# A transformer block on one core: in the last matrix product, the transfer of the second weight sum is put first and its use one product later, and product 2 is summed in two PSUM banks of its own

## The chip, the cores and the metric

The kernel runs on one core of a Trainium2 chip. The metric is the device time of one execution in microseconds (us); smaller is better. A profile adds one execution with every instruction's start, length and waits.

## The reference

One layer of a decoder block, batch 1, 512 tokens, width 1024, everything in float32:

```python
h = rmsnorm(x, norm_attn_g)
[q | k | v | u_pool | u_gate] = h @ w_in
a = diff_attention(q, k, v, ...)          # 8 heads, causal
p = multiscale_pool(u_pool, ...)
x = x + (sigmoid(g_A) * a + sigmoid(g_P) * p) @ w_out
z = square(relu(rmsnorm(x, norm_mlp_g) @ w_up))     # w_up 1024 x 4096
x = x + z @ w_down                                   # w_down 4096 x 1024
out = rmsnorm(x, final_norm_g)
```

The change lies in the last three lines.

## The kernel before

**Precision.** Every float32 product is made of three passes of TensorE: an operand is split into a high part (`hi`, a cast to the narrower float32r by ScalarE) and a low part (`lo`, the remainder, by VectorE), and hi x hi, lo x hi and hi x lo are summed. So each weight block needs a cast on ScalarE (ACT, line 112) and a subtraction on VectorE (DVE, line 113) before TensorE (PE) may use it, and so does each block of z (lines 694 and 695).

**The MLP in four quarters.** The 4096 hidden columns are done in quarters `q` = 0 to 3: `up(q)` computes z of a quarter (quarter 0 by the plain `up_plain`), `down(q)` multiplies it with its quarter of `w_down` and adds it to `x1`. Each is a 2 x 2 block product by a scheme of Strassen's kind: seven products of sums of blocks in place of eight. The products are named m1 to m7 in the code, and each takes a weight form: m5 takes S1, m1 takes A11, m2 takes A12, m6 takes S2, m3 takes S4, m7 takes S3, m4 takes A22. The text says "product 5" for m5, and so on. A product of `down` is 24 matmuls of 128 x 512 (two banks, four slices, three passes).

**Weights.** `weights` makes the weight forms of a quarter. Four blocks are in HBM, each as two halves of 128 x 1024 (512 KB), numbered by `c`. Blocks 0 and 1 are loaded over SyncE's queue (SP) into `r11` (buffers `wr`) and `al` (`wal`). Their sum `ga` (`wga`, line 665) is the form S1, the first weight sum. Other forms are made in place by DMAs that add while they write, issued on GpSimd's queue (POOL, line 645): `al` + block 3 is S3, `ga` + block 3 is S2 (the second weight sum), and `ga` + block 2 is A22's. Before such an addition may start, the low part of the form that is there must have been taken out of the buffer. Blocks 2 (A12) and 3 (S4) are loaded as they are into the two `wr` buffers, so each load waits until the buffer's last user is through.

```python
for n, form in enumerate(order):
    if n == 1:
        plus(al, 3)
    ...
        w = parts(ga, f"t{form}", None if form == S1 else first[-1])
        if form != A22:
            plus(ga, {S1: 3, S2: 2}[form])
```

In a group name, `wh_dt` and `wl_dt` are the high and low part of a weight sum of `down` (`wh_ut` of `up`), `wh_db` and `wl_db` those of a block used as it is. A name with numbers says which: `wh_dt5_1_0` is the form S2 (code 5) of quarter 1, half 0; `wh_db21_1_0` is block 2 (for product 2) of quarter 1, half 0. `z0`, `z1`, `z4`, `z5` are z for A11, A12, S1, S2.

**PSUM.** `acc` hands out the eight banks in turn. A product's two banks are added to `x1` by DVE (`to_x1`, line 837); products 1, 6, 7 and 4 go on in the same two banks (`ma`), 5 and 3 in another pair (`mc`), and product 2 takes a fresh pair in each quarter and is added to `x1` in each.

**Order.** The program is written product by product, and a scheduler with a timeline of its own then sets the order of the instructions on each engine; `after(later, earlier)` only adds a rule of order. On the chip, each engine runs its own list in that order: an instruction that waits holds up all that stand behind it on its engine.

Of the kernel before, what the change touches and what calls it, by code (L numbers as in the profile page):

```python
# [15 lines left out]
ALU = mybir.AluOpType  # L16
# [35 lines left out]
def block_kernel(ctx, tc, xT, x_tok, gains, pos, consts, w_in, w_v, w_pool, w_out, w_up, w_dn, out):  # L52
# [5 lines left out]
    def after(later, earlier):  # L58
        tc.add_manual_dep(
            later.ins, earlier.ins.name,  # L60
            mybir.DependencyInfo(mybir.DependencyClass.NoSync, mybir.DependencyReason.DATA), reason="issue order",
        )
# [252 lines left out]
    acc = Rot((0, 1, 2))  # L315
# [310 lines left out]
        parts(S4)  # L626


    nparts = [0]
    first = []  # L630
    zform = {}

    def weights(src, q, nm, order):

        def raw(b, tag="wr", pool=wp):
            tiles = [pool.tile([P, 1024], F32, tag=tag, name=f"{tag}_{nm}{b}_{q}_{c}", bufs=2) for c in range(2)]
            if b is not None:
                for c in range(2):
                    nc.sync.dma_start(out=tiles[c], in_=src[q, b, c])
            return tiles  # L640

        def plus(tiles, b):

            for c in range(2):
                G.dma_start(out=tiles[c], in_=src[q, b, c], accum_op=ALU.add)  # L645

        def parts(rs, b, hold=None):

            third = nparts[0] % 3 == 2
            nparts[0] += 1  # L650
            out_ = []
            for c in range(2):
                hi, lo = (
                    (bk if third else wp).tile([P, 1024], F32R, tag=t_ + "b" * third, name=f"{t_}_{nm}{b}_{q}_{c}", bufs=2 if third else 4)
                    for t_ in ("wh", "wl")
                )
                cast = split_w(rs[c], hi, lo, eng=V)
                if hold:
                    after(cast, hold)
                out_.append((hi, lo))  # L660
            return out_

        r11, al, ga = raw(0), raw(1, "wal", bk), raw(None, "wga", bk)
        for c in range(2):
            V.tensor_tensor(out=ga[c], in0=r11[c], in1=al[c], op=ALU.add)  # L665
        for n, form in enumerate(order):
            if n == 1:
                plus(al, 3)
            if form == A11:
                yield parts(r11, "b11")  # L670
            elif form == A12:
                yield parts(raw(2), "b21")
            elif form == S4:
                yield parts(raw(3), "b22")
            elif form == S3:
                yield parts(al, "t3", first[-1])
            else:
                w = parts(ga, f"t{form}", None if form == S1 else first[-1])
                if form != A22:
                    plus(ga, {S1: 3, S2: 2}[form])  # L680
                yield w

    def halves(r):
# [22 lines left out]
    def up_plain(q):  # L706

        rows = state["rows"]
        for c in range(2):
            for par in range(2):  # L710
                w = []
                for kh in range(2):
                    tiles = load_w(w_up[q, 2 * kh + par, c], f"up{q}_{kh}{par}{c}")
                    cast = split_w(*tiles, eng=V)
                    if c + par:
                        after(cast, rows)
                    w.append(tiles[1:])
                pa = [acc(f"pu{q}_{par}{c}_{p}") for p in range(2)]
                for ts in ((0, 1), (1, 2)) if c + par == 0 else ((0, 2),):
                    for p in range(2):  # L720
                        a_ = pa[p][:, ts[0] * HS : ts[1] * HS]
                        for part in range(2):
                            for k in range(NK):
                                c_ = slice((p * 4 + k % 4) * P, (p * 4 + k % 4) * P + P)
                                for i in range(2 - part):
                                    T.matmul(a_, lhsT=w[k // 4][part][:, c_], rhs=gab[k // 4][:, ts[0] : ts[1], i, k % 4, :],  # L726
                                             start=k + i + part == 0, stop=part == 1 and k == NK - 1)
                for p in range(2):
                    r = rawz[:, (0, 1)[par] : (4, 3)[par] : (3, 1)[par], 2 * c + p, :]
                    A.activation(out=r, in_=pa[p].rearrange("p (a t) -> p a t", a=2), func=AF.Relu)  # L730
                    A.activation(out=r, in_=r, func=AF.Square)
                if c + par == 0:
                    forms_h2()
            sub(4, 2, 3, c)
            zsplit(q, S1, R[4], c)
            zsplit(q, A11, R[0], c)
            sub(4, 4, 0, c, True)
            zsplit(q, S2, R[4], c)
            zsplit(q, A12, R[1], c)
            sub(1, 4, 1, c, True)  # L740
            sub(0, 0, 3, c)
        zsplit(q, S4, R[1])
        zsplit(q, S3, R[0])
        zsplit(q, A22, R[2])

    def up(q):

        W = weights(w_up, q, "u", (A11, S1, S2, S3, A22, A12, S4))

        def product(form, name, onto=None):  # L750
            w, pa = next(W), onto or [acc(f"u{name}{q}_{i}") for i in range(2)]
            rh, rl = gf[form]
            first.append(None)
            for i in range(2):
                hi, lo = w[i]
                for p in range(2):
                    a_ = pa[i][:, p * HS : p * HS + HS]
                    for k in range(4):
                        c = slice((p * 4 + k) * P, (p * 4 + k) * P + P)
                        m = T.matmul(a_, lhsT=hi[:, c], rhs=rh[:, k, :], start=p + k == 0 and onto is None, stop=False, skip_group_check=True)  # L760
                        first[-1] = first[-1] or m
                        T.matmul(a_, lhsT=hi[:, c], rhs=rl[:, k, :], start=False, stop=False, skip_group_check=True)  # L762
                    for k in range(4):
                        c = slice((p * 4 + k) * P, (p * 4 + k) * P + P)
                        T.matmul(a_, lhsT=lo[:, c], rhs=rh[:, k, :], start=False, stop=k == 3, skip_group_check=True)  # L765
            return pa

        def keep(pa, r):
            for a_, r_ in zip(bank_view(pa), halves(r)):
                A.copy(out=r_, in_=a_)  # L770

        def join(pa, r):
            for a_, r_ in zip(bank_view(pa), halves(r)):
                V.tensor_tensor(out=r_, in0=a_, in1=r_, op=ALU.add)

        def z_of(r, sign, pa=None):
            for i, r_ in enumerate(halves(r)):
                A.activation(out=r_, in_=bank_view(pa)[i] if pa else r_, func=AF.Relu, scale=sign)
                A.activation(out=r_, in_=r_, func=AF.Square)

        ma = product(A11, "m1")
        keep(ma, R[0])
        mc = product(S1, "m5")
        keep(mc, R[2])
        product(S2, "m6", onto=ma)
        keep(ma, R[1])
        product(S3, "m7", onto=ma)
        join(ma, R[2])
        z_of(R[2], -1.0)
        product(A22, "m4", onto=ma)  # L790
        z_of(R[3], 1.0, ma)
        sub(4, 2, 3)
        zsplit(q, S1, R[4])
        join(product(A12, "m2"), R[0])
        z_of(R[0], 1.0)
        zsplit(q, A11, R[0])
        sub(4, 4, 0, neg=True)
        zsplit(q, S2, R[4])
        product(S4, "m3", onto=mc)
        join(mc, R[1])  # L800
        z_of(R[1], -1.0)
        zsplit(q, A12, R[1])
        sub(1, 4, 1, neg=True)
        zsplit(q, S4, R[1])
        sub(0, 0, 3)
        zsplit(q, S3, R[0])
        zsplit(q, A22, R[2])

    def down(q):
        W = weights(w_dn, q, "d", (S1, A11, S2, A12, S4, S3, A22))  # L810
        last = q == 3

        def mms(a_, form, w, a, cols, start):
# [11 lines left out]
        def product(form, name, onto=None):  # L825
            w, pa = next(W), onto or [acc(f"d{name}{q}_{a}") for a in range(2)]
            first.append(None)
            for a in range(2):
                m, _ = mms(pa[a], form, w, a, (0, 512), onto is None)
                first[-1] = first[-1] or m  # L830
            return pa

# [16 lines left out]
        to_x1(mc, 1, 1)  # L849
        ma = product(A11, "m1")  # L850
        to_x1(ma, 0, 0)
        product(S2, "m6", onto=ma)
        if last:
            after(gmul, first[-1])
        to_x1(ma, 0, 1)
        to_x1(product(A12, "m2"), 0, 0)
        complete(0, 0)
        product(S4, "m3", onto=mc)
        to_x1(mc, 0, 1)
        if last:  # L860
# [104 lines left out]
```

## Time and profile before

| what | value |
|---|---|
| median of 3 runs | 704.28 us (702.53 to 705.14) |
| profiled execution, its time | 700.6 us |
| profiled execution, its span | 698.8 us |
| TensorE busy in the span | 678.3 us (97%) |
| VectorE / ScalarE / GpSimd busy | 519.1 / 446.1 / 161.8 us |
| mean granted TensorE clock | 0.991 |
| read from HBM | 100.30 MB, 147 GB/s over the span |

The span runs from the first to the last instruction; the time of the same execution is 1.8 us longer. TensorE's busy time counts a matmul from its issue to its modelled end, so that neighbours overlap: 97% busy leaves little room, and what there is shows as stretches in which TensorE waits or runs at a lower granted clock. The MLP's four `down` parts begin at about 402, 480, 563 and 646 us.

### The profile page before, as it was taken

The numbers are of one execution on the slowest core, as the hardware profiler recorded it, in microseconds if no ns is written. First come the engines' busy times: TensorE is split into PE (matmuls) and PEld (weight loads), VectorE is DVE, ScalarE is ACT, GpSimd is POOL, SyncE is SP. The second block draws the span as 40 slices with busy tenths as digits, with TensorE's granted clock in tenths as the row PEclk, the third lists the DMA queues.
The fourth block names the chain that finished last, engine by engine and source line by source line (L and its number), as shares of the span: only waits on it lengthen the run. The fifth ranks groups of instructions, "written<-read, shape, count | busy, mean of one in ns | idle before, by whom it ended". The sixth has DMA issues, their size and how long they took to land.

```text
span 698.8 us, 9783 instructions
## 1 busy us (share of the span) xinstructions
PE 678.3 (97%) x3590; PEld 581.6 (83%) x3590; DVE 519.1 (74%) x853; ACT 446.1 (64%) x723; POOL 161.8 (23%) x159
## 2 busy tenths in 40 slices
PE   8999999999999999999999999999899999999795
PEld 7888878887888887888888888999689978899584
DVE  6943977688788865965489789468985789567796
ACT  8554487877888789874356665366545765267555
POOL 6101634264346524610000100102010110101000
PEclk9999999999999999999999999999999999999999
DMA  8534573416346274584133774879468784876723
GB/s 276 170 106 124 133 151 111 110 60 151 103 117 151 69 174 91 121 240 170 42 121 99 141 206 129 173 219 209 128 185 186 194 183 164 187 182 162 178 61 120
DMA packets 30863, 103.03 MB, mean 147 GB/s; under 512 B 3808, under 2 KB 4448, under 8 KB 30816
## 3 DMA queue, kind: packets, MB, share of 16 engines
q1 hardware_dynamic: 21456, 68.59, 28.7%
q0 software_dynamic: 9216, 33.56, 27.5%
q8 instruction: 28, 0.46, 0.3%
q10 hardware_dynamic: 144, 0.26, 0.1%
q14 instruction: 19, 0.16, 0.1%
HBM read 100.30 MB, written 2.10 MB: 147 GB/s over the span
## 4 chain that ended last, share of the span: by engine, by line
PE 68%; DVE 13%; DMA 8%; ACT 6%; issue 4%; POOL 1%; SPq 0%; ACTq 0%; POOLq 0%; DVEq 0%
PE pu L726 5%; PE dm L821 5%; PE dm L822 5%; PE dm L819 5%; DMA wga_dNone<-w_dn 3%; PE um L760 3%; PE um L762 3%; PE um L765 3%; PE v L220 2%; PE v L221 2%; PE v L222 2%; DMA wga_uNone<-w_up 2%; PE po L557 2%; PE po L558 2%; PE po L559 2%
## 5 line engine op out<-in xcount | busy, mean ns | idle before, releaser
L821 PE MATMUL dm<-wh_dt,z 128*128 128x512 f32 (+1 forms) x128 | 49.6, 387 | 0.1
L822 PE MATMUL dm<-wl_dt,z 128*128 128x512 f32 (+1 forms) x128 | 49.2, 386 | 0.0
L819 PE MATMUL dm<-wh_dt,z 128*128 128x512 f32 (+1 forms) x128 | 48.9, 388 | 0.3 <-ACT z L694 0.3
L837 DVE TENSOR_TENSOR x<-x,dm 128x512 f32<-128x512 f32 x54 | 36.3, 681 | 15.0 <-PE dm L822 14.9
L112 ACT CAST wh_ut<-wga_uNone 128x1024 fp32r<-128x1024 f32 x18 | 18.9, 1050 | 43.3 <-DMA wga_uNone<-w_up 32.5
L376 ACT ACTIVATE p<-p,st 128x128 f32<-128x128 f32 (+3 forms) x64 | 35.7, 559 | 12.4 <-DVE st L372 11.8
L821 PE MATMUL dm<-wh_db,z 128*128 128x512 f32 x96 | 39.3, 417 | 4.3 <-DVE z L695 4.3
L819 PE MATMUL dm<-wh_db,z 128*128 128x512 f32 x96 | 38.2, 409 | 3.8 <-ACT wh_db L112 3.1
L112 ACT CAST wh_dt<-wga_dNone 128x1024 fp32r<-128x1024 f32 x24 | 24.9, 1047 | 22.7 <-DMA wga_dNone<-w_dn 17.6
L113 DVE TENSOR_TENSOR wl_ut<-wga_uNone,wh_ut 128x1024 fp32r<-128x1024 f32 x18 | 22.0, 1223 | 23.2 <-ACT wh_ut L112 23.2
L113 DVE TENSOR_TENSOR wl_dt<-wga_dNone,wh_dt 128x1024 fp32r<-128x1024 f32 x24 | 28.9, 1219 | 13.3 <-ACT wh_dt L112 13.3
L645 POOL DMA_DIRECT2D wal_d<-w_dn x8 | 6.9, 864 | 135.3 <-DVE wga_dNone L665 118.9
L822 PE MATMUL dm<-wl_db,z 128*128 128x512 f32 x96 | 38.0, 408 | 0.0
L112 ACT CAST wh_db<-wr_d 128x1024 fp32r<-128x1024 f32 x24 | 25.0, 1045 | 19.2 <-DMA wr_d<-w_dn 17.8
L760 PE MATMUL um<-gss,wh_ut 128*128 128x256 f32 x144 | 36.1, 283 | 0.0
L762 PE MATMUL um<-gss,wh_ut 128*128 128x256 f32 x144 | 36.1, 283 | 0.0
L113 DVE TENSOR_TENSOR wl_db<-wr_d,wh_db 128x1024 fp32r<-128x1024 f32 x24 | 29.1, 1218 | 7.2 <-PE pu L726 4.5
L695 DVE TENSOR_TENSOR z<-rawz,z 128x1024 fp32r<-128x1024 f32 (+1 forms) x32 | 34.2, 1084 | 0.0
L726 PE MATMUL pu<-gab,wh_up 128*128 128x512 f32 (+1 forms) x160 | 31.7, 349 | 0.6 <-DVE gab L596 0.4
L372 DVE CUSTOM_DVE_ANT_0 p<-s,mask 128x128 f32<-128x128 f32 (+3 forms) x64 | 29.8, 482 | 2.0 <-PE s L371 2.0
L694 ACT CAST z<-rawz 128x1024 fp32r<-128x1024 f32 (+1 forms) x32 | 29.3, 937 | 2.9 <-PE dm L822 1.2
L726 PEld LDWEIGHTS pu<-gab,wh_up 128*128 128x128 f32 x160 | 25.9, 189 | 5.0 <-DVE gab L596 0.8
(310 smaller groups left out, 2235.2 us busy)
## 6 DMA issues: line engine op xcount, KB each, us to landing
wr_d<-w_dn SPq DMA_DIRECT2D x24, 512.0 KB, 3.6
wr_u<-w_up SPq DMA_DIRECT2D x18, 512.0 KB, 3.8
wga_dNone<-w_dn POOLq DMA_DIRECT2D x16, 512.0 KB, 5.7
wga_uNone<-w_up POOLq DMA_DIRECT2D x12, 512.0 KB, 7.9
wr_q<-w_in SPq DMA_DIRECT2D x8, 512.0 KB, 3.3
wr_k<-w_in SPq DMA_DIRECT2D x8, 512.0 KB, 3.7
wr_ga<-w_in SPq DMA_DIRECT2D x8, 512.0 KB, 3.3
wr_gp<-w_in SPq DMA_DIRECT2D x8, 512.0 KB, 3.3
```

The lines of the kernel that those rows point to most:

```text
L112: ins = A.copy(out=hi[:, sl], in_=raw[:, sl])
L113: (eng or G).tensor_tensor(out=lo[:, sl], in0=raw[:, sl], in1=f(hi)[:, sl], op=ALU.subtract)
L372: V.tensor_tensor_reduce(out=pr[:, c, :N], in0=s_[:, :N], in1=mask[:, S - N :], scale=-0.125, scalar=-NEG, op0=ALU.add, op1=ALU.min, accum ...
L376: A.activation(out=pr[:, c, :N], in_=pr[:, c, :N], func=AF.Exp, scale=-1.0, bias=st[:, c : c + 1], accum_out=st[:, 2 + c : 3 + c])
L695: V.tensor_tensor(out=z[:, 1, sl], in0=r[:, sl], in1=f(z[:, 0, sl]), op=ALU.subtract)
L726: T.matmul(a_, lhsT=w[k // 4][part][:, c_], rhs=gab[k // 4][:, ts[0] : ts[1], i, k % 4, :], start=k + i + part == 0, stop=part == 1 and k ...
L760: m = T.matmul(a_, lhsT=hi[:, c], rhs=rh[:, k, :], start=p + k == 0 and onto is None, stop=False, skip_group_check=True)
L762: T.matmul(a_, lhsT=hi[:, c], rhs=rl[:, k, :], start=False, stop=False, skip_group_check=True)
L819: m = T.matmul(a_, lhsT=zh, rhs=hi[:, sl], start=p == 0 and start, stop=False, skip_group_check=True)
L821: T.matmul(a_, lhsT=zl, rhs=hi[:, sl], start=False, stop=False, skip_group_check=True)
L822: end = T.matmul(a_, lhsT=zh, rhs=lo[:, sl], start=False, stop=p == 3, skip_group_check=True)
L837: V.tensor_tensor(out=xs, in0=xs, in1=pa[a], op=(ALU.add, ALU.subtract)[n])
```

## The change

In `weights`, which `up` and `down` share, the addition of block 3 to `ga` (which makes the second weight sum) is issued ahead of the addition of block 3 to `al`; `after` ties that order. In `down`, product 2 (A12) is written ahead of product 6 (S2), and in `up` the split of z for A12 ahead of that for S2. Product 2's two banks are now banks 6 and 7, kept for it alone: it is summed over the four quarters there and added to `x1` once, in the last quarter; `acc` turns over the six others.

```diff
+    acc = Rot(tuple(range(6)))
+    m2 = [bank(6 + a, f"dm2_{a}") for a in range(2)]
...
         def plus(tiles, b):
-            for c in range(2):
-                G.dma_start(out=tiles[c], in_=src[q, b, c], accum_op=ALU.add)
+            return [G.dma_start(out=tiles[c], in_=src[q, b, c], accum_op=ALU.add) for c in range(2)]
...
         for n, form in enumerate(order):
-            if n == 1:
-                plus(al, 3)
...
                 w = parts(ga, f"t{form}", None if form == S1 else first[-1])
                 if form != A22:
-                    plus(ga, {S1: 3, S2: 2}[form])
+                    adds = plus(ga, {S1: 3, S2: 2}[form])
+                if form == S1:
+                    for i in plus(al, 3):
+                        after(i, adds[1])
                 yield w
...
# up_plain
             zsplit(q, A11, R[0], c)
+            zsplit(q, A12, R[1], c)
             sub(4, 4, 0, c, True)
             zsplit(q, S2, R[4], c)
-            zsplit(q, A12, R[1], c)
...
# up
         zsplit(q, A11, R[0])
-        sub(4, 4, 0, neg=True)
-        zsplit(q, S2, R[4])
         product(S4, "m3", onto=mc)
         join(mc, R[1])
         z_of(R[1], -1.0)
         zsplit(q, A12, R[1])
+        sub(4, 4, 0, neg=True)
+        zsplit(q, S2, R[4])
...
# down
-        W = weights(w_dn, q, "d", (S1, A11, S2, A12, S4, S3, A22))
+        W = weights(w_dn, q, "d", (S1, A11, A12, S2, S4, S3, A22))
...
-                m, _ = mms(pa[a], form, w, a, (0, 512), onto is None)
+                m, _ = mms(pa[a], form, w, a, (0, 512), onto is None or onto is m2 and q == 0)
...
         ma = product(A11, "m1")
         to_x1(ma, 0, 0)
-        product(S2, "m6", onto=ma)
+        product(A12, "m2", onto=m2)
         if last:
             after(gmul, first[-1])
+            to_x1(m2, 0, 0)
+        complete(0, 0)
+        product(S2, "m6", onto=ma)
         to_x1(ma, 0, 1)
-        to_x1(product(A12, "m2"), 0, 0)
-        complete(0, 0)
         product(S4, "m3", onto=mc)
```

What the scheduler makes of it shows at three places, all in quarter 1 of `down` (quarter 2 has the same rows). First POOL's list, the six additions of the quarter, before:

```order
L645 DMA wal_d1_1_0_4475<-w_dn 128x1024
L645 DMA wga_dNone_1_0_4479<-w_dn 128x1024
L645 DMA wal_d1_1_1_4476<-w_dn 128x1024
L645 DMA wga_dNone_1_1_4480<-w_dn 128x1024
L645 DMA wga_dNone_1_0_4479<-w_dn 128x1024
L645 DMA wga_dNone_1_1_4480<-w_dn 128x1024
```

and now:

```order
L646 DMA wga_dNone_1_0_4477<-w_dn 128x1024
L646 DMA wga_dNone_1_1_4478<-w_dn 128x1024
L646 DMA wal_d1_1_0_4473<-w_dn 128x1024
L646 DMA wal_d1_1_1_4474<-w_dn 128x1024
L646 DMA wga_dNone_1_0_4477<-w_dn 128x1024
L646 DMA wga_dNone_1_1_4478<-w_dn 128x1024
```

Both additions to `wga` that make the second weight sum now stand ahead of both additions to `wal`. Then ACT's list, from the cast of z for A11 (`z0`) on, before (the rows 778 and 779 are ReLU and square of z):

```order
L694 CAST z0_1_4384<-rawz_2995 128x1024
L778 ACTIVATE rawz_2995<-rawz_2995 128x512
L112 CAST wh_dt5_1_0_4559<-wga_dNone_1_0_4479 128x1024
L112 CAST wh_dt5_1_1_4563<-wga_dNone_1_1_4480 128x1024
L779 ACTIVATE rawz_2995<-rawz_2995 128x512
L778 ACTIVATE rawz_2995<-rawz_2995 128x512
L694 CAST z5_1_4388<-rawz_2995 128x1024
L779 ACTIVATE rawz_2995<-rawz_2995 128x512
L112 CAST wh_db21_1_0_4599<-wr_d2_1_0_4595 128x1024
L694 CAST z1_1_4457<-rawz_2995 128x1024
L112 CAST wh_db21_1_1_4603<-wr_d2_1_1_4596 128x1024
```

and now, from the row ahead of ReLU and square:

```order
L112 CAST wh_db21_1_0_4561<-wr_d2_1_0_4557 128x1024
L781 ACTIVATE rawz_2995<-rawz_2995 128x512
L782 ACTIVATE rawz_2995<-rawz_2995 128x512
L781 ACTIVATE rawz_2995<-rawz_2995 128x512
L697 CAST z0_1_4382<-rawz_2995 128x1024
L782 ACTIVATE rawz_2995<-rawz_2995 128x512
L781 ACTIVATE rawz_2995<-rawz_2995 128x512
L782 ACTIVATE rawz_2995<-rawz_2995 128x512
L112 CAST wh_db21_1_1_4565<-wr_d2_1_1_4558 128x1024
L697 CAST z1_1_4451<-rawz_2995 128x1024
L697 CAST z5_1_4455<-rawz_2995 128x1024
L112 CAST wh_dt5_1_0_4593<-wga_dNone_1_0_4477 128x1024
```

The casts of the second weight sum (`wh_dt5`) have moved from ahead of z for A12 (`z1`) to behind it, and the first cast of product 2's weights (`wh_db21_1_0`) has moved ahead of `z0`. In quarter 3 that cast stays behind `z0`, and `wh_dt5` moves as here. Third, PE's list at the end of product 1 of quarter 1, before:

```order
L819 MATMUL dm11_1_4532<-wh_db11_1_1_4527,z0_1_4384 128x512
L821 MATMUL dm11_1_4532<-wh_db11_1_1_4527,z0_1_4384 128x512
L822 MATMUL dm11_1_4532<-wl_db11_1_1_4528,z0_1_4384 128x512
L819 MATMUL dm21_0_4607<-wh_db21_1_0_4599,z1_1_4457 128x512
L819 MATMUL dm21_1_4608<-wh_db21_1_0_4599,z1_1_4457 128x512
L821 MATMUL dm21_0_4607<-wh_db21_1_0_4599,z1_1_4457 128x512
```

and now:

```order
L822 MATMUL dm11_1_4530<-wh_db11_1_1_4525,z0_1_4382 128x512
L824 MATMUL dm11_1_4530<-wh_db11_1_1_4525,z0_1_4382 128x512
L825 MATMUL dm11_1_4530<-wl_db11_1_1_4526,z0_1_4382 128x512
L822 MATMUL dm2_0_3357<-wh_db21_1_0_4561,z1_1_4451 128x512
L822 MATMUL dm2_1_3358<-wh_db21_1_0_4561,z1_1_4451 128x512
L824 MATMUL dm2_0_3357<-wh_db21_1_0_4561,z1_1_4451 128x512
```

Here nothing moved: in quarters 1 to 3 the scheduler had put product 2 right behind product 1 already before the change. Only its banks are others.

## The prediction

> **What bounds the kernel now.** I read the page's first part, then the waits by engine, then stretches of the `down` parts.
>
> ```profile
> PE 678.3 (97%) x3590; PEld 581.6 (83%) x3590; DVE 519.1 (74%) x853; ACT 446.1 (64%) x723; POOL 161.8 (23%) x159
> PE dm L821 <- DVE z L695: 4.3, 3, 1.9
> PE dm L819 <- ACT wh_db L112: 3.1, 1, 3.1
> ACT wh_dt L112 <- DMA wga_dNone<-w_dn: 17.6, 5, 5.2
> ```
>
> TensorE is the bound, so only its own waits are worth anything. The two largest (total us, times, longest) are in `down`: it waits for z's low part three times and once for a cast of weights. Idle time is not all that such a wait costs. A `down` product is 24 matmuls, so I set product 1 of quarters 1, 2 and 3 beside the product 2 that follows it (stretch, its length, PE busy, granted clock, DMA share, GB/s):
>
> ```profile
> 485.71:491.15 5.44, 5.44 (x25) 1.00 0.70 109
> 491.16:501.14 9.98, 7.62 (x25) 0.83 0.69 186
> 568.73:574.17 5.44, 5.44 (x25) 1.00 0.78 126
> 574.18:583.32 9.14, 7.32 (x25) 0.81 0.62 190
> 652.36:657.80 5.44, 5.44 (x25) 1.00 0.66 153
> 657.81:669.18 11.37, 7.73 (x25) 0.85 0.65 153
> 494.50:497.90 3.40, 3.40 (x10) 0.59 0.76 258
> ```
>
> The same 24 matmuls take 5.44 us undisturbed, and 9.98, 9.14 and 11.37 us in product 2. The excess is 4.54, 3.70 and 5.93 us, 14.17 us in all. Some of it is idle, the rest a lower granted clock: 0.59 in the 3.4 us behind the wait of quarter 1. Who is late there shows ACT's timeline, with PE's two waits behind it (start, length, engine, line):
>
> ```profile
> 486.30 1.05 ACT L112 CAST wh_dt<-wga_dNone 128x1024 fp32r<-128x1024 f32 x1 [5.25 <-DMA wga_dNone<-w_dn]
> 487.26 0.63 ACT L779 ACTIVATE rawz<-rawz 128x512 f32<-128x512 f32 x1
> ...
> 490.73 1.04 ACT L694 CAST z<-rawz 128x1024 fp32r<-128x1024 f32 x1
> 491.81 0.73 PE L819 MATMUL dm<-wh_db,z 128*128 128x512 f32 x2 [0.50 <-ACT z L694]
> 494.40 0.50 PE L821 MATMUL dm<-wh_db,z 128*128 128x512 f32 x1 [1.86 <-DVE z L695]
> ```
>
> ACT stands still for 5.25 us at the second half of `wh_dt5`, because the addition that makes this weight sum has not landed. ReLU, square and cast of z for A12 (490.73) stand behind it in ACT's list, though product 2 needs nothing of that sum. PE pays at 491.81 and 494.40. Why the sum is late, POOL's timeline shows. Behind it stand SP's issue of the first load for product 2, the page's row of all additions (packets, MB, share of the DMA engines' time), and landings (us from the issue, the last figure): the addition issued at 476.86, one with POOL's queue to itself, the load issued at 474.32, and an undisturbed load:
>
> ```profile
> 469.62 0.86 POOL L645 DMA_DIRECT2D wal_d<-w_dn  x1 [16.83 <-DVE wga_dNone L665]
> 471.72 0.86 POOL L645 DMA_DIRECT2D wga_dNone<-w_dn  x1 [1.25 <-DVE wl_dt L113]
> 472.86 0.86 POOL L645 DMA_DIRECT2D wal_d<-w_dn  x1 [0.27 <-DVE wga_dNone L665]
> 476.86 0.86 POOL L645 DMA_DIRECT2D wga_dNone<-w_dn  x1 [3.14 <-DVE wl_dt L113]
> 474.32 0.33 SPq L639 DMA_DIRECT2D wr_d<-w_dn  x1
> ...
> q0 software_dynamic: 9216, 33.56, 27.5%
> wga_dNone<-w_dn POOLq DMA_DIRECT2D x1, 512.0 KB, 9.4
> wga_dNone<-w_dn POOLq DMA_DIRECT2D x1, 512.0 KB, 5.2
> wr_d<-w_dn SPq DMA_DIRECT2D x1, 512.0 KB, 9.5
> wr_d<-w_dn SPq DMA_DIRECT2D x1, 512.0 KB, 3.2
> ```
>
> The addition behind two to `wal` takes 9.4 us, one alone 5.2. All additions together, 64 of 512 KB, take 27.5% of 698.8 us on the DMA engines, 3.0 us each, which is my pace for a row of them. Quarters 2 and 3 look alike.
>
> **The change part by part, and the sum.**
>
> *Additions reordered.* POOL's list now has both `wga` additions first. Each still waits for the low part taken out of `wga` (the releaser in their rows), so neither can start earlier than 471.72 and 476.86. The first then lands at about 471.72 + 5.2 = 477, the second at 476.86 + 5.2 = 482, at worst 1.5 us later beside a load, not at 486.3. The `wal` additions come behind: two at 3.0 us each put the last at about 488 to 490. In `down` nothing reads `wal` before product 7, which starts 16 us (three products of 5.44) after product 2's start at 491.16, so I take 0; in `up` there is a case for a loss, the last rival.
>
> *Casts reordered.* z for A12 and its weights no longer stand behind `wh_dt5`. PE's list shows no gain of its own, since product 2 already followed product 1 there. The gain is that its operands come in time. In quarter 1, ACT ends the first cast of product 2's weights at about 479.5 (landing 474.32 + 3.2, and up to 1 us more beside the addition still in flight), then ReLU, square, ReLU and `z0` bring it to about 483, three more ReLU and squares (0.63 each) to 485, the second weight cast and `z1` to 487.5, the low part on DVE to about 489. Product 2 begins at 491.16. I take its excess as gone in quarters 1 and 2: 4.54 + 3.70. `wh_dt5` then ends near 490; product 6 wants it at 496.6. For each quarter the ends are nothing and the whole excess.
>
> *Quarter 3.* The excess of 5.93 goes too, but this part is short of DVE:
>
> ```profile
> 646.00:691.00 45.00, 37.31 (x55) 0.96 0.41 101
> 651.57 1.05 ACT L112 CAST wh_dt<-wga_dNone 128x1024 fp32r<-128x1024 f32 x1 [4.24 <-DMA wga_dNone<-w_dn]
> 655.38 1.05 ACT L112 CAST wh_dt<-wga_dNone 128x1024 fp32r<-128x1024 f32 x1 [2.76 <-DMA wga_dNone<-w_dn]
> ```
>
> ACT stood for 7 us here. DVE is busy 37.31 of 45.00 us; with 5.93 us less it would be 37.31 of 39.07, 95%. I take 4.8 and leave 1.1 to a queue that has little room; the ends are 0 and 5.93.
>
> *Product 2's own banks.* Six additions to `x1` fall away (two in each of quarters 0 to 2). By this row they take 6 x 0.681 = 4.1 us off DVE:
>
> ```profile
> L837 DVE TENSOR_TENSOR x<-x,dm 128x512 f32<-128x512 f32 x54 | 36.3, 681 | 15.0 <-PE dm L822 14.9
> 481.09 0.68 DVE L774 TENSOR_TENSOR rawz<-um,rawz 128x512 f32<-128x512 f32 x1
> 481.69 1.22 DVE L702 SCALAR_TENSOR_TENSOR rawz<-rawz 128x1024 f32<-128x1024 f32 x1
> ```
>
> They lie beside TensorE, and DVE waits 15.0 us for PE ahead of this group, so I take 0 (ends 0 and 4.1). Six banks in turn for eight: product 1 of `down` now takes the banks of product 3's sum in `up`, which the addition at 481.09 reads. It ends at 481.8 and product 1 begins at 485.7, so 0; with DVE held up it costs what is beyond 3.9 us.
>
> The sum: 4.54 + 3.70 + 4.8 = 13.0 us off the profiled execution, 700.6 to 687.6. The runs' median is 3.7 us above that execution; I take the same 13.0 off it: 704.28 - 13.0 = **691.3 us**.
>
> [...]
>
> **The rivals.**
>
> *The wait moves to product 1.* The first cast of product 2's weights now stands ahead of `z0` in quarters 1 and 2. If its load lands as late as now, 474.32 + 9.5 = 483.8, then cast (1.05), low part (1.2), join (0.68), subtraction and `z0`'s low part (1.22 each) end at 489.2, where product 1 wants it at about 486.4: 2.8 us idle and some 2 of slow clock, all that quarter 1 loses now. Quarter 2 likewise, quarter 3 not. The time would be 704.28 - 4.8 = 699.5. Against it: at 474.32 only one addition is now in POOL's queue, not three. [...]
>
> *DVE binds quarter 3.* If 95% cannot be had and only 1 of the 5.93 us goes, the time is 704.28 - 4.54 - 3.70 - 1 = 695.0. For it speaks that DVE's list is in order and the casts it waits for come from ACT; against it, that ACT's 7 us held DVE up too, so that part of its rows comes earlier.
>
> *Nothing changes:* the loads and additions are the same bytes, DMA decides and the waits go to other casts, 704.3. Against it: ACT's 5.25 us and 7 us are waits for a sum that the next product does not use.
>
> *Slower.* In `up`, `wal` is read by product 7, and its casts now wait for additions that stand last:
>
> ```profile
> 437.91 0.86 POOL L645 DMA_DIRECT2D wga_uNone<-w_up  x1 [1.77 <-DVE wl_ut L113]
> 451.22 2.01 ACT L112 CAST wh_ut<-wal_u 128x1024 fp32r<-128x1024 f32 x2
> 454.05 1.05 ACT L112 CAST wh_ub<-wr_u 128x1024 fp32r<-128x1024 f32 x1 [0.33 <-PE um L762]
> 457.20 0.28 PE L760 MATMUL um<-gab,wh_ub 128*128 128x256 f32 x1
> ```
>
> The cast at 454.05 stands behind those of `wal`, and PE wants it at 457.20. Four additions from 437.91, the first 5.2 us and then about 3 each, put the last `wal` at 452; the point from which PE waits is 457.2 less two casts (2.1) and a copy (0.6), 454.5. Landing at 458.5 would cost 4 us and about 2 of clock in each of three quarters, 18 us: 704.28 - 13 + 18 = 709.
>
> **How the numbers follow.** A measurement can tell about 0.5% here, 3.5 us: faster means below 700.8. The forecast has 0.60, DVE 0.20, the wait at product 1 0.10, nothing 0.05, slower 0.05. The first two are faster for certain, the third mostly; so 0.87 faster, 0.08 same, 0.05 slower. The range goes from 687.5 (704.28 - 14.17 = 690.1, less the 1.75 by which the lowest run lies under the median, and some of the 4.1) to 698.5, past the DVE case and short of the third; the two inside hold 0.80.
>
> **What would show it.** Right: no DMA wait of ACT above about 1 us ahead of `z1` in `down`; product 2 in 5.4 to 6 us in three quarters with a clock of 1.00; 48 additions to `x1` in the group that has 54. Wrong: PE waiting for `z0` with ACT at `wh_db` for a load (rival one), PE waiting for DVE after 660 us (rival two), PE waiting in `up` for `wh_ub` or `wh_ut` (the last). A second `wga` addition still at 9 us would refute the first step.

## The result, and the profile after

The changed kernel takes 686.9 us (median of four runs, 686.13 to 687.41) against 704.7 us (702.53 to 706.49): a ratio of 0.9748, 95% interval 0.9718 to 0.9777. That is 17.8 us less; 13.0 were forecast, and the time lies 0.6 us below the range. Two repeats on other chips gave 686.7 against 702.6 (0.9765, 0.9738 to 0.9791) and 687.2 against 702.6 (0.9786, 0.9751 to 0.9822). The profiled executions are 700.6 before and 686.13 after, 14.5 us apart.

The first row is from the page's first part (busy time of each engine). Behind it stand the rows of PE's waits that concern `down` (the two largest of before, 4.3 and 3.1 us, are gone), then the group of additions to `x1`:

```profile
PE 670.8 (98%) x3590; PEld 577.3 (84%) x3590; DVE 516.1 (75%) x847; ACT 447.7 (65%) x723; POOL 162.2 (24%) x159
PE dm L824 <- DVE z L698: 0.3, 1, 0.3
PE dm L822 <- ACT z L697: 0.2, 1, 0.2
L840 DVE TENSOR_TENSOR x<-x,dm 128x512 f32<-128x512 f32 x48 | 32.1, 680 | 8.7 <-PE dm L825 8.6
```

Product 2 of quarters 1, 2 and 3 (stretch, length, busy PE, PEld, DVE, ACT, POOL, clock, DMA share, GB/s):

```profile
490.83:496.27 5.44, 5.44 (x25) 4.50 (x24) 5.44 (x6) 4.16 (x6) 0.86 (x1) 1.00 0.43 101
569.29:574.73 5.44, 5.44 (x25) 4.51 (x24) 5.44 (x6) 4.20 (x5) 1.10 (x2) 1.00 0.43 93
649.23:654.67 5.44, 5.44 (x25) 4.50 (x24) 5.44 (x7) 5.44 (x6) 1.65 (x2) 1.00 0.49 129
```

All three take 5.44 us at full clock, where they took 9.98, 9.14 and 11.37. That is 14.17 of the 14.5 us by which the two profiled executions differ.

ACT's timeline of quarter 1 shows that the waits for DMA have not gone; they stand elsewhere. The last two rows are POOL's and DVE's:

```profile
478.21 1.05 ACT L112 CAST wh_db<-wr_d 128x1024 fp32r<-128x1024 f32 x1 [1.51 <-DMA wr_d<-w_dn]
480.89 1.04 ACT L697 CAST z<-rawz 128x1024 fp32r<-128x1024 f32 x1
487.18 1.05 ACT L112 CAST wh_db<-wr_d 128x1024 fp32r<-128x1024 f32 x1 [3.54 <-DMA wr_d<-w_dn]
488.13 2.00 ACT L697 CAST z<-rawz 128x1024 fp32r<-128x1024 f32 x2
490.04 2.00 ACT L112 CAST wh_dt<-wga_dNone 128x1024 fp32r<-128x1024 f32 x2
476.12 0.86 POOL L646 DMA_DIRECT2D wga_dNone<-w_dn  x1 [4.65 <-DVE wl_dt L113]
489.40 1.22 DVE L698 TENSOR_TENSOR z<-rawz,z 128x1024 fp32r<-128x1024 f32 x1
```

ACT now waits 3.54 us at the second cast of product 2's own weights, whose load (issued at 477.58, landed at 487.10) shares the DMA engines with three additions and another load. z1 stands behind it all the same, but the cast of z1 comes at 488.13 in place of 490.73, its low part at 489.40, ready at 490.62, and product 2 starts at 490.83. The wait is two thirds of the old one (5.25 us); what counts is that z1 is ready 0.2 us before product 2 starts.

### The profile page after: what moved, and what is told of

It reads as the page before. It is cut to its first block, busy times and chain, and to the rows that moved or that the text cites. A ratio compares the mean times of both kernels' runs of the same rounds, so it can differ in the third digit from the quotient of the medians.

```text
span 684.4 us, 9772 instructions
## 1 busy us (share of the span) xinstructions
PE 670.8 (98%) x3590; PEld 577.3 (84%) x3590; DVE 516.1 (75%) x847; ACT 447.7 (65%) x723; POOL 162.2 (24%) x159
## 3 DMA queue, kind: packets, MB, share of 16 engines
q0 software_dynamic: 9216, 33.56, 27.5%
## 4 chain that ended last, share of the span: by engine, by line
PE 58%; issue 18%; DVE 10%; DMA 9%; ACT 3%; POOL 1%; SPq 0%; POOLq 0%; DVEq 0%; ACTq 0%
PE pu L729 6%; DMA wga_uNone<-w_up 5%; PE dm L824 4%; PE dm L825 4%; PE dm L822 4%; PE gp L131 2%; PE gp L132 2%; PE gp L135 2%; PE po L557 2%; PE po L559 2%; PE po L558 2%; PE q L131 2%; PE q L132 2%; PE k L135 2%; PE k L132 2%
## 5 line engine op out<-in xcount | busy, mean ns | idle before, releaser
L646 POOL DMA_DIRECT2D wga_dNone<-w_dn x16 | 13.8, 865 | 232.4 <-DVE wl_dt L113 148.2
L113 DVE TENSOR_TENSOR wl_db<-wr_d,wh_db 128x1024 fp32r<-128x1024 f32 x24 | 29.2, 1220 | 14.2 <-ACT wh_db L112 9.3
L840 DVE TENSOR_TENSOR x<-x,dm 128x512 f32<-128x512 f32 x48 | 32.1, 680 | 8.7 <-PE dm L825 8.6
L824 PE MATMUL dm<-wh_db,z 128*128 128x512 f32 x96 | 37.0, 389 | 0.0
L822 PE MATMUL dm<-wh_db,z 128*128 128x512 f32 x96 | 36.2, 390 | 0.2 <-ACT z L697 0.2
L112 ACT CAST wh_dt<-wga_dNone 128x1024 fp32r<-128x1024 f32 x24 | 24.7, 1048 | 9.5 <-DMA wga_dNone<-w_dn 3.5
L729 PEld LDWEIGHTS pu<-gab,wh_up 128*128 128x128 f32 x160 | 25.9, 189 | 5.0 <-DVE gab L596 0.8
```

The source lines that it names most:

```text
L112: ins = A.copy(out=hi[:, sl], in_=raw[:, sl])
L113: (eng or G).tensor_tensor(out=lo[:, sl], in0=raw[:, sl], in1=f(hi)[:, sl], op=ALU.subtract)
L822: m = T.matmul(a_, lhsT=zh, rhs=hi[:, sl], start=p == 0 and start, stop=False, skip_group_check=True)
L824: T.matmul(a_, lhsT=zl, rhs=hi[:, sl], start=False, stop=False, skip_group_check=True)
L840: V.tensor_tensor(out=xs, in0=xs, in1=pa[a], op=(ALU.add, ALU.subtract)[n])
```

## The experiments

The change has three parts that can be made one without the other. I ran each by itself, and the first two together. "Before" is the kernel before on the same chip.

| kernel | median, us (range) | before | ratio (95% interval) | product 2's excess, us |
|---|---|---|---|---|
| additions alone | 690.5 (689.0 to 693.3) | 703.0 | 0.984 (0.981 to 0.987) | 0.2 |
| order of casts and products alone | 694.5 (693.6 to 698.1) | 703.0 | 0.989 (0.986 to 0.992) | 1.5 |
| both, no own banks | 688.5 (687.3 to 693.0) | 703.0 | 0.982 (0.978 to 0.985) | 0.0 |
| the same, another chip | 689.6 (688.2 to 691.7) | 702.6 | 0.980 (0.977 to 0.983) | 0.2 |
| own banks alone | 700.5 (697.4 to 702.7) | 702.6 | 0.996 (0.994 to 0.999) | 11.1 |
| all three | 686.7 (685.1 to 688.4) | 702.6 | 0.977 (0.974 to 0.979) | 0.0 |

The last column is what the product 2 of quarters 1 to 3 took above 3 x 5.44 us in the profiled execution, one for each row. In three profiles of the kernel before it is 14.2, 17.8 and 20.8.

**Additions alone.** The edit is the hunks of `plus` and of the `after` in `weights`; the lists of ACT and PE stay those of before.

```diff
-            if n == 1:
-                plus(al, 3)
...
-                    plus(ga, {S1: 3, S2: 2}[form])
+                    adds = plus(ga, {S1: 3, S2: 2}[form])
+                if form == S1:
+                    for i in plus(al, 3):
+                        after(i, adds[1])
```

> Before, with the additions reordered alone (both to wga ahead of both to wal); the order of casts and products and the banks stay as before. Theory A, the late sum is the cause: the sum lands about 4 us earlier (a little over 5 us after its issue in place of 9.4), ACT's wait at wh_dt5 falls from 4 to 5 us to about 1 in each quarter, and product 2 comes down to 6 us or less in all three: 688 to 693 us. Theory B, the place of the cast is the cause: z1 still stands behind wh_dt5 and waits for whatever lands last, so half or more of the excess stays: 696 us or more. The load of product 2's weights, which an addition beside it also slows, keeps quarter 3's 3 us in either.

It took 690.5, and product 2's excess fell from 14 us to 0.2. ACT's timeline of quarter 1, `wh_dt5` and then z1:

```profile
484.57 1.05 ACT L112 CAST wh_dt<-wga_dNone 128x1024 fp32r<-128x1024 f32 x1 [1.18 <-DMA wga_dNone<-w_dn]
488.99 1.05 ACT L694 CAST z<-rawz 128x1024 fp32r<-128x1024 f32 x1
```

The wait at `wh_dt5` is 1.18 us in place of 5.25, although z1 still stands behind it. So the stall needs the late sum, as theory A has it, and theory B, by which half or more of the excess stays, falls. The 3 us that I expected to stay in quarter 3 for the load went too.

**Order alone.** The edit is the hunks of `up_plain`, `up` and `down`, with a fresh pair of banks for product 2:

```diff
-        W = weights(w_dn, q, "d", (S1, A11, S2, A12, S4, S3, A22))
+        W = weights(w_dn, q, "d", (S1, A11, A12, S2, S4, S3, A22))
...
-        product(S2, "m6", onto=ma)
+        m2 = product(A12, "m2")
+        to_x1(m2, 0, 0)
+        complete(0, 0)
+        product(S2, "m6", onto=ma)
         to_x1(ma, 0, 1)
-        to_x1(product(A12, "m2"), 0, 0)
-        complete(0, 0)
```

> Before, with products and casts reordered alone (product 2 and z1 ahead of product 6 and the second weight sum); the additions alternate as before, and product 2 takes fresh banks in each quarter. Theory B: wh_dt5 now waits behind z1, where nothing of product 2 stands behind it, so product 2 runs in 5.4 to 6 us although the sum still lands 9 us after its issue: 687 to 690 us. Theory A: the late sum then makes product 6 wait, about 1 to 3 us in each quarter, 694 to 698. A third: the load for product 2 lands late behind three additions, its cast stands ahead of z0, and product 1 waits: about 699.

It took 694.5. Product 2 is nearly clean, though the sum is as late as ever: in quarter 2 its second addition took 11.5 us (557.40 to 568.93). So the stall of product 2 also needs the place of the cast, and it goes when either is taken away. Product 6 did not wait for the sum (5.44 us in quarter 2), so theory A's half of this expectation failed. The wait has moved to product 1, as the third case has it. Quarter 2, ACT and then PE at product 1 (its first matmuls, and the stretch of the product), in a profiled execution of 698.1, the longest of the eight:

```profile
565.29 1.05 ACT L112 CAST wh_db<-wr_d 128x1024 fp32r<-128x1024 f32 x1 [6.92 <-DMA wr_d<-w_dn]
567.30 1.03 ACT L693 CAST z<-rawz 128x1024 fp32r<-128x1024 f32 x1
568.38 0.73 PE L818 MATMUL dm<-wh_db,z 128*128 128x512 f32 x2 [2.38 <-ACT z L693]
570.52 0.79 PE L820 MATMUL dm<-wh_db,z 128*128 128x512 f32 x1 [1.41 <-DVE z L694]
568.38:578.37 9.99, 8.58 (x25) 6.51 (x26) 9.99 (x11) 7.66 (x10) 0.74 (x1) 0.66 0.32 105
```

ACT waits 6.92 us for the load of product 2's weights, which is in flight together with three additions, and z0 stands behind that cast. This is the prediction's first rival, which gave 699.5. In the changed kernel the same cast waits 1.51 us in quarter 1 and 0.82 in quarter 2: the additions put in order are what keeps this rival from coming true.

**Both, without the own banks.**

```diff
-    acc = Rot(tuple(range(6)))
-    m2 = [bank(6 + a, f"dm2_{a}") for a in range(2)]
...
-        product(A12, "m2", onto=m2)
+        m2 = product(A12, "m2")
         if last:
             after(gmul, first[-1])
-            to_x1(m2, 0, 0)
+        to_x1(m2, 0, 0)
```

> The changed kernel without product 2's own banks: both reorderings, eight banks in turn, x1 added to in each quarter (54 additions again). Theory: the banks are worth nothing, since the six additions (4.1 us of DVE) lie beside TensorE: 687 us, within 0.2% of the changed kernel. Rival: DVE binds quarter 3 or the joins of up, and the additions cost 1 to 4 us: 688 to 691.

It took 688.5 on one chip; beside the changed kernel on another chip I ran it again:

> The changed kernel without product 2's own banks, for times on the same chip as the changed kernel. It had 688.5 against 686.9, but on another chip. Theory: the six additions lie beside TensorE, and the two agree within 0.1%, 0.7 us. Rival: the banks are worth the 1.6 us seen.

> The changed kernel, unchanged, beside the next ones. The first times (686.1 to 687.4, four runs) hold: 686 to 688 us, with a narrow spread, while the kernel before spreads over 8 us or more on the same chip, since what varies there is product 2's stall, which the changed kernel has not. Rival: the narrow spread was luck of four runs, and the changed kernel also spreads over 5 us or more.

689.6 (688.2 to 691.7) against 686.7 (685.1 to 688.4): the own banks are worth about 2.9 us, and my zero for them is refuted. The ranges of the runs barely overlap. The changed kernel ranged over 3.3 us in five runs (4.0 in a later six), the kernel before over 9.6, so its narrow spread was not luck, but wider than the first four runs had it. Alone, on top of before, the banks bring 2.1 us:

> Before, with product 2's own banks alone (summed over the quarters in banks 6 and 7, six banks in turn, six additions fewer); casts, products and transfers in the order of before. Theory: nothing, 702 to 704 us, product 2's excess 14 to 18 us as before. Rival: two additions fewer in each quarter let DVE make z's low part earlier, and 1.5 to 4 us of the stall go: 699 to 702.

Here the rival held: 700.5, a small effect (ratio 0.994 to 0.999).

**Where the time goes without the own banks.** PE's waits in its second profile are in other places than product 2 of `down`. PE's two largest rows in the MLP, and then, from the timeline, its wait at the start of quarter 3's `down` and the stretch behind it:

```profile
PE um L761 <- ACT wh_ub L112: 1.0, 1, 1.0
PE dm L820 <- ACT z L695: 1.9, 2, 1.7
641.68 0.73 PE L820 MATMUL dm<-wh_dt,z 128*128 128x512 f32 x2 [1.69 <-ACT z L695]
641.68:646.50 4.82, 4.60 (x12) 3.15 (x13) 4.61 (x6) 3.32 (x5) 0.00 (x0) 0.65 1.03 254
```

The first wait is at product 2 of quarter 3's `up` (619.58): weights of that `up` are late, and behind them the start of its `down`, where the clock falls to 0.65 too. The additions back in the changed kernel, without touching the banks:

```diff
-                m, _ = mms(pa[a], form, w, a, (0, 512), onto is None or onto is m2 and q == 0)
+                m, _ = mms(pa[a], form, w, a, (0, 512), onto is None or onto is m2)
...
         if last:
             after(gmul, first[-1])
-            to_x1(m2, 0, 0)
+        to_x1(m2, 0, 0)
```

> The changed kernel, with banks 6 and 7 for product 2 as in it, but started and added to x1 in every quarter: the six additions are back, the banks are not touched. What the own banks were worth (689.6 without against 686.7 with them) is either the additions or the banks in turn. Theory, the additions: they stand in DVE's list ahead of the low parts of wh_dt3, whose end lets SP load the next quarter's wal, and so hold up the chain of weights in up by 1.2 us or more: 689 to 690 us, with PE waiting near 619 for wh_ub and 2 to 4 us at the start of quarter 3's down. Rival, the banks (eight in turn make a join or an addition wait): 686.7.

690.3, on a chip without a run of the changed kernel: this speaks for the six additions, not the banks, and `adds_up` below settles it. I then thought of their place ahead of `wh_dt3` (the casts of S3, product 7's weight sum), and in the kernel without own banks put them behind it:

```diff
         product(S3, "m7", onto=ma)
+        for m in late:             # m2's two additions of this quarter
+            after(m, first[-1])
```

> The changed kernel without product 2's own banks, with its two additions of quarters 0 to 2 put behind the first matmul of product 7, and so behind the low parts of wh_dt3. As many additions as without the own banks, only later. Theory, the place of the additions is the cost: 687 us, as with the own banks. Rival, the work itself: 689 to 690.

691.0, so that place is not the cause. In the changed kernel I moved another instruction of DVE, the low part of z for S3 (`z6`), out from before the low parts of `wh_dt3`:

```diff
         product(S3, "m7", onto=ma)
+        if not last:
+            after(zlow[S3], low[0])   # z6's low part behind that of wh_dt3
```

> The changed kernel, with the low part of z6 in quarters 0 to 2 put behind the low parts of wh_dt3. No work is saved; the loads of the next quarter's wal start 1.1 us earlier. Theory, the chain from there to the start of the next down binds what is left at quarter 3's start (1.3 to 1.6 us): 685.7 to 686.3. Rival: the changed kernel is past the point where this chain counts, 686.7, or the late z6 makes product 7 wait, 688.

687.9: nothing gained. But both edits leave the moved work ahead of the first weight sum of the next `up`. From product 2 of quarter 2 to the first addition of that `up` (which waits for the sum's low part), each kernel's stretch has this row; the columns are as above, the third number in front of a bracket is DVE, and the number in the bracket counts its instructions. In this order: the changed kernel (second repeat), both without banks, the additions back, `adds_late`:

```profile
569.12:594.13 25.01, 25.01 (x125) 21.26 (x124) 25.01 (x27) 14.09 (x14) 1.73 (x3) 1.00 0.61 173
570.57:597.72 27.15, 27.15 (x139) 22.81 (x138) 27.15 (x30) 15.48 (x16) 1.73 (x3) 1.00 0.60 163
570.91:597.87 26.96, 26.96 (x139) 22.83 (x138) 26.96 (x30) 15.31 (x16) 1.73 (x2) 1.00 0.60 164
571.51:599.00 27.49, 27.49 (x142) 23.60 (x141) 27.49 (x31) 15.14 (x16) 1.73 (x2) 1.00 0.60 170
```

DVE is busy for the whole of each stretch, 25.01 of 25.01 us, though its share of the span is 75%. If this is the cause, the order inside such a stretch does not matter, and each instruction more moves its end. The test is to put the two additions past it, into the next `up`, where DVE waits for ACT:

```diff
 # up, next quarter
         product(S3, "m7", onto=ma)
+        while late:
+            after(late.pop(), first[-1])
```

> The changed kernel without own banks for product 2, its two additions of quarters 0 to 2 held until the first matmul of product 7 in the next up, where DVE waits for ACT. As many additions as in the runs of 689.6 to 691.0. Theory, the stretch: DVE has no idle time from about 570 to 598, and what stands there moves the whole chain of weights of the next up; outside it the additions are free: 686.7 to 687.5. Rival, work anywhere: 689.5 or more.

It took 686.1 (684.8 to 688.5; ratio 0.977, 0.973 to 0.980), with all 54 additions and without own banks: as the changed kernel, which took 687.2 on the same chip. The rival, work anywhere, falls; the stretch stands. The second test takes two other additions, those of product 3, out of it in the changed kernel:

```diff
-        to_x1(mc, 0, 1)
+        to_x1(mc, 0, 1, not last)      # True holds the two additions back
...
 # up, next quarter, when the first weight sum's parts are made
+            while form == S1 and late:
+                after(late.pop(), low[0])
```

> The changed kernel, with the two additions of product 3 (1.4 us) in quarters 0 to 2 held until behind the low parts of the next up's first weight sum. Theory, the stretch: the chain of the next up comes 1.2 to 1.4 us earlier, and of the 1.3 to 1.6 us that PE still loses at the start of quarter 3's down, most goes: 685.3 to 686. Rival: what is left there is bound by the loads alone, 686.7; or the additions hold up up's product 5, which takes their banks, 688.

> The changed kernel once more, for times on the same chip: 686 to 688 us.

685.2 (684.1 to 687.2) against 687.2 (685.9 to 690.0) for the changed kernel on the same chip. The intervals of the two ratios overlap (0.972 to 0.979, 0.975 to 0.982), so the 2 us are likely, not certain; it is the fastest version here. The stretches of the last two:

```profile
569.13:593.96 24.83, 24.83 (x123) 21.09 (x122) 24.83 (x26) 13.92 (x14) 1.73 (x2) 1.00 0.60 171
569.23:592.53 23.30, 23.30 (x110) 19.56 (x109) 23.30 (x24) 13.49 (x14) 1.73 (x3) 1.00 0.63 177
```

Stretch and median time go together, in three groups: 23.3 us has 685.2; 24.8 and 25.0 have 686.1 and 687.2; 27.0, 27.2 and 27.5 have 690.3, 689.6 and 691.0. Each stretch is from one profiled execution, and the medians come from three chips, so within a group the order says nothing. The other profiles fit, with one exception: 24.7 twice for the changed kernel, 25.9 for the moved `z6` (687.9), 26.5 in the first run without banks (688.5); but 24.3 for the next kernel (688.1), which loses elsewhere. A single execution can also lose behind the stretch: the profiled one of `adds_up` took 688.5, the longest of its six, with a wait of 1.54 us at the start of quarter 3's `down` and a granted clock of 0.65 in the 4.8 us from its end.

**A rule that lost.** What PE still loses in the changed kernel is 1.3 to 2.1 us at the start of quarter 3's `down`, where ReLU and square of the z for product 5 stand behind casts of the first weight sum, which waits for a load. I held those casts back:

```diff
-                w = parts(ga, f"t{form}", None if form == S1 else first[-1])
+                w = parts(ga, f"t{form}", (state["r3"] if nm == "d" and q == 3 else None) if form == S1 else first[-1])
```

> The changed kernel with one more rule: in quarter 3, the casts of the first weight sum stand behind ReLU and square of the z that product 5 needs. In the profile of the changed kernel PE loses 1.3 us at the start of quarter 3's down, waiting for z4 and z0, whose ReLU and squares stand behind two casts that wait for a load. Theory: that loss goes, 1 to 1.5 us: 685.3 to 686. Rival: the low parts of the first weight sum, and so the additions for the second, come 1 to 2 us later, and the wait moves to product 1 or 2: 687 or more.

688.1 against 686.7 on the same chip, so nothing is gained (the intervals, 0.976 to 0.981 and 0.974 to 0.979, overlap). PE now waits there for DVE, and later for DVE's row statistics at the end:

```profile
PE dm L825 <- DVE z L698: 1.7, 1, 1.7
PE dm L823 <- DVE st L551: 0.5, 1, 0.5
```

**Why the median moved by more than the profiled pair.** Two more profiles of the kernel before:

> The kernel before, unchanged, for a second profile and more times. Its runs lay 1.9 to 5.9 us above the profiled 700.6, those of the changed kernel 0 to 1.3 us above theirs. If the difference is the same stall being longer in other executions, the profile shows a time T with product 2's excess over 5.44 us in quarters 1 to 3, summed, equal to 14.2 + (T - 700.6) within 0.7 us. Rival: the rest of the kernel varies, and the excess stays at 14 whatever T is.

> The kernel before once more, for a third profile: product 2's excess over 5.44 us in quarters 1 to 3 was 14.2 us at 700.6 and 17.8 at 704.2. If its time T varies by that stall alone, the excess here is 14.2 + (T - 700.6) within 1 us.

The first has 704.17 us (the median of its twelve runs is 702.7). Its product 2 in quarters 1 to 3:

```profile
491.87:504.21 12.34, 8.62 (x25) 6.47 (x25) 9.88 (x12) 6.90 (x8) 0.00 (x0) 0.72 0.64 170
577.23:587.53 10.30, 7.33 (x25) 5.50 (x25) 9.12 (x11) 6.18 (x7) 0.00 (x0) 0.83 0.63 171
661.32:672.76 11.44, 7.75 (x25) 5.44 (x25) 9.84 (x12) 7.48 (x9) 0.86 (x1) 0.85 0.68 155
```

The excess is 34.08 - 16.32 = 17.76 us: 3.59 more than in the profile that I predicted from, for 3.57 us more time. That the match is so close is partly luck: quarter 0's `down` also took 0.88 us more, and what stands ahead of it 0.88 us less. The second was a single execution of 709.6, above all timed ones, with an excess of 20.8 where the expectation gave 23.2, so that expectation failed: of the 9.0 us more, 6.6 are in product 2, and 2.4 are not. PE waits in two further places there: 1.27 us in quarter 0's `down` and 1.09 us at the start of quarter 3's. So the stall explains the difference near the median, and most of it above.

## Why the prediction was right or wrong

- **What bounds the kernel, and why product 2 is late: right.** The excess of 14.17 us in the profile is gone to the last hundredth, and the additions alone take 14 of it away. It was right to price the slow clock with the idle time: PE was not busy for 2.36, 1.82 and 3.64 us of the three stretches of product 2, 7.82 in all; the other 6.35 us went too, and the clock was 0.59 in the 3.4 us behind 1.86 us of idle time.
- **The step that failed: "I take the same 13.0 off it".** The sum was made on a profiled execution 3.7 us faster than the median and carried over unchanged, as if those 3.7 us were something else. They are mostly the same stall, longer: 17.76 us at 704.17. Taken off 704.28, that gives 686.5; 686.9 was measured. The forecast saving was 4.8 us short (13.0 of 17.8): 3.6 us are this step, 1.1 us what was left to DVE in quarter 3. The three runs shown lay all above the profiled one, which should have raised the question. It is one profile near the median that shows this size.
- **The term for product 2's own banks was mis-sized:** zero taken, 2.9 us measured (689.6 against 686.7), inside the ends of 0 and 4.1. Without the banks the two medians, 688.5 and 689.6, lie inside the stated range; with them the time lies just below it. "They lie beside TensorE, and DVE waits 15.0 us for PE ahead of this group" is the wrong row to rest on. Of these 15.0 us, 4.6 are three waits of 1.5 to 1.6 us for the stalled product 2 itself, and go with the stall; 7.3 are two waits of 3.64 us (524.85 and 607.03) at `down`'s last products. In the 25 us that follow product 2, DVE of the changed kernel has no idle time. In before, the cast for product 2 of quarter 3's `up` ended 1.6 us ahead of PE (623.70, 625.28), which itself came late; without the stall and without the banks PE waits 1.0 us for it. So the banks are no term beside the excess: they keep some of it from being given back. That the stall covered this chain is read from these two profiles; no run tests it alone, and the 2.1 us of the banks on top of before say that the cover was not complete.
- **Additions reordered: right, but its own sign of being wrong came true in quarter 3.** The second addition of quarter 1, issued at 476.12, took 5.5 us. That of quarter 3 took 9.3 (633.40 to 642.71), which by the sign that I had set refutes the step there. The sign was the wrong one, since it took the time from issue to landing, and what counts is the landing beside the use. Before, this addition took 13.1 us (642.20 to 655.30). It now lands 5.8 us after the start of z0's cast, where it was 9.5, and the additions alone took quarter 3's excess away as well.
- **Casts reordered: right in result, with less room than worked out.** z1 was to be done at 487.5 and its low part at 489; they were done at 489.2 and 490.6, since the second load landed late. "No DMA wait of ACT above about 1 us ahead of z1" was wrong (3.54 us).
- **Quarter 3: 5.93 us, not 4.8.** The 1.1 us left to DVE's queue were not needed, and the rival that DVE binds quarter 3 did not come in that place. DVE does bind, but from product 2 to the next `up`, and PE pays a quarter later.
- **The wait at product 1** has 0.10 and did not come, but the order alone brings it about, at 694.5. **The slower case** has a trace of truth: without the banks PE waits 1.0 us for `wh_ub` in quarter 3's `up`, where the rival had 4. Ahead of that cast ACT waits 1.44 us for the second addition to `wal`, as the rival has it, and then 2.11 us for the sum in `wga`, which is the last to hold it up. In the changed kernel (second repeat) ACT has the same two waits, 1.47 and 1.50 us, and PE waits for none of it.

## What to carry to other kernels

A stall that hangs on transfers can differ from one execution to the next (14.2, 17.8 and 20.8 us here), and the profiled one is a single draw. Where the runs lie above it, ask whether the stall is longer in them, and scale its price before it is taken off.

An engine's share of the span says nothing about a stretch. Count its idle time between the two events that a chain runs through. Where there was none, two additions of 0.68 us moved out of the stretch shortened it by 1.7 us and the run by about 2, and two moves within it gained nothing. When a stall is removed, look at what is late next; here it was a chain on another engine, worth a sixth of the gain.

## What the runs showed of the hardware

The clock's price after a wait is not a function of the wait's length alone. Here are two waits of 1.7 us at the start of quarter 3's `down` and what followed, first with the banks left out (1.69 us, its stretch with a clock of 0.65 shown above), then in the kernel with the held casts:

```profile
639.64 0.50 PE L825 MATMUL dm<-wh_dt,z 128*128 128x512 f32 x1 [1.69 <-DVE z L698]
639.64:644.50 4.86, 4.86 (x21) 4.05 (x22) 2.81 (x3) 0.82 (x2) 0.00 (x0) 1.00 1.03 261
```

The same 1.69 us cost nothing further here: 21 matmuls in 4.86 us at a clock of 1.00, against 12 in 4.82 at 0.65. Nor is it the place in the program: at the first matmuls of the same product, a wait of 1.62 us in the kernel with the moved `z6` left the clock at 1.00 for the next 4.8 us (mean of the execution 0.998), and one of 1.54 us in `adds_up` brought it to 0.65 (mean 0.996). What decides between the two, no run here shows.
